# Loads asked for one head ahead, kq doubled on ScalarE, and value products spread over two pairs, in the attention of an encoder kernel

## The chip, the cores and the metric

The kernel runs on one core of a Trainium2 chip. The metric is the device time of one execution in microseconds (us). A core has four compute engines, each with its own queue in program order: TensorE (PE), VectorE (DVE), ScalarE (ACT) and GpSimd (POOL). A fifth, SyncE (SP), only issues DMA transfers. Engines wait for each other by semaphores; an instruction that waits holds everything behind it in its queue.

## The reference

Two encoder layers on 1024 positions of width 1024; attention and a convolution branch run side by side, then a gated feed-forward part with a short convolution:

```python
for l in range(2):
    p = rmsnorm(x, g_mix[l]) @ w_in[l]
    q = (rmsnorm(p[..., :384], g_q[l]) @ w_uq[l]).reshape(b, s, 8, 64 + 32)
    kv = (rmsnorm(p[..., 384:640], g_kv[l]) @ w_ukv[l]).reshape(b, s, 8, 64 + 64)
    q_nope, q_rope = q[..., :64], apply_rope(q[..., 64:])
    k_nope, v = kv[..., :64], kv[..., 64:]
    k_rope = apply_rope(p[..., 640:672])              # one for all heads
    sc = (q_nope . k_nope + q_rope . k_rope) / sqrt(96)   # per head, 1024 x 1024
    y_attn = softmax(sc) @ v
    u = silu(layernorm(dwconv31(a * sigmoid(gate))))
    x = x + concat(y_attn, u) @ w_o[l]
    z = dwconv3(rmsnorm(x, g_ffn[l]) @ w_up[l])
    x = x + (silu(z_gate) * z_value) @ w_down[l]
return rmsnorm(x, g_final)
```

## The kernel before

All instructions are put into the engines' queues by one Python program; its order is the order of each queue. Values of full precision are kept as a high and a low half (16-bit, or a rounded 32-bit pair), so that a product of two is several 16-bit products.

The change is in `attention`, which runs once per layer: about 190 of 2220 us, twice. Each of 8 heads has 8 **query tiles** of 128 queries, taken as 4 **pairs** (p = 0 to 3), 32 pairs in all. For a pair the steps are:

- `begin` and `scores`: for each of the two tiles a **whole product** of four 128x512 matmuls (line 1860, tiles k and q), and for both a **rest product** of four 32-row matmuls (L1867), which adds what is left of the rotary part. Its operand kq has to lie in rows 0 to 63 and again in rows 64 to 127; `again` copies it (L2066). The scores of a tile lie in a wide PSUM buffer, of which there are two.
- `largest`: the row maximum on DVE (L1878); `expo`: the exponential on ACT (L1886), which also sums the rows.
- `turn(pair, c)`, c = 0 to 3: four PE transposes (L1904) into a PSUM bank, of both tiles' probabilities for two key tiles; `upper` (ACT, L1912) writes the high half pt, `lower` (DVE, L1916) the low half. There are four such banks, shared with other users.
- `values(group, c)`: a **group** is two pairs, a half head. Two matmuls (L1932) of high halves for each c, and after c = 3 eight 64-column ones (L1937) for the low halves; then the output y is taken out by ACT (L1943) and DVE (L1944).
- `sums(h)`: reciprocal on DVE (L1954), written to memory (sd, L1955) and read back broadcast (rb, L1956), both by SP; POOL multiplies y by rb (L1965) `Y_DELAY` tiles later, and y is split into high and low (ys) on ACT (L233) and POOL (L235).

The main loop begins the scores of pair + 1 and turns `pair`. In between it issues side work by an agenda of due times (`others`): taps of the convolution on POOL (L2169 to L2174), sums of the layer norm (lns, L2180), output weights wo (L1000, L214, L215). `products(n)` issues one value step per tile: two in each pair, and in every second pair the eight closing matmuls.

The transfers of a head's k, q and kq are issued on SP by `load_head`, through the helper `move` (L159), from memory copies kd, qd and qrd. kq has three buffers, k and q two each. `load(h + 1)` stands in `begin` at p = 1 of head h. The tables `ROWS_FIRST` to `ROWS_LATE` say when the eight row tiles of v are made (`rows`, L1833).

Of the kernel before, what the change touches and what calls it, by code (L numbers as in the profile page):

```python
# [64 lines left out]
FFN_BANKS = (2, 4)  # L65
SIDE_TIME = 56
TOTAL_TIME = 57
Y_DELAY = 3
SUMS_AT = 8
Y_LAST = 4  # L70
Y_SPLIT = 8
# [79 lines left out]
class Encoder:  # L151
# [421 lines left out]
    def project(self, l, carry):  # L573
# [205 lines left out]
        def query_rope(i):  # L779
            p = ps[f"u{i}"]  # L780
            c, s = self.blk(f"rc{l}_{i}"), self.blk(f"rs{l}_{i}")
            for o, t in ((c, st["cos"]), (s, st["sin"])):
                nc.vector.tensor_tensor(out=by_parity(o), in0=in_order(p), in1=in_order(t), op=ALU.mult)
            st["rope", i] = c, s
            yield 2.44, 0.0
            if i == 0:
                return
            (c1, s1), (c2, s2) = st.pop(("rope", 0)), st.pop(("rope", 1))
            nc.vector.tensor_tensor(out=c1, in0=c1, in1=s2, op=ALU.subtract)
            nc.vector.tensor_tensor(out=c2, in0=c2, in1=s1, op=ALU.add)  # L790
            two = [self.blk(f"qr{l}_{i}", F16, (128, 2, T)) for i in range(2)]
            for hl, o in zip(two, (c1, c2)):
                nc.scalar.copy(out=hl[:, 0], in_=o)
            yield 2.5, 1.0
            for i, (hl, o) in enumerate(zip(two, (c1, c2))):
                nc.vector.scalar_tensor_tensor(out=hl[:, 1], in0=o, scalar=1.0, in1=hl[:, 0], op0=ALU.mult, op1=ALU.subtract)
                yield 1.25, 0.0
                self.move(qrd[i].rearrange("h d p t -> (h d) p t"), hl)
            for i, hl in enumerate(two):
                mine = hl[0:HALF]  # L800
                for e in range(2):
                    self.move(heads[0][2][e * ROPE + i * HALF:e * ROPE + (i + 1) * HALF], mine[:, 0, HALVES[e]])
                for p in range(2):
                    at = NOPE + i * ROPE + p
                    self.move(heads[0][0][at:at + ROPE - 1:2, 1], mine[:, p])

        def query(j):
            n = self.blk(f"qn{l}_{j}")
            nc.vector.tensor_tensor(out=by_parity(n), in0=in_order(ps[f"n{j}"]), in1=in_order(st["rq"]), op=ALU.mult)  # L809
            hl = self.blk(f"qns{l}_{j}", F16, (128, 2, T))  # L810
            nc.scalar.copy(out=hl[:, 0], in_=n)
            yield 1.22, 1.5
            nc.vector.scalar_tensor_tensor(out=hl[:, 1], in0=n, scalar=1.0, in1=hl[:, 0], op0=ALU.mult, op1=ALU.subtract)
            for h in range(DIRECT if j == 0 else 0):
                mine = hl[h * NOPE:(h + 1) * NOPE]
                self.move(heads[h][0][NOPE:128, 0], mine[:, 0])
                self.move(heads[h][0][0:NOPE], mine)
            if j:
                self.move(qd[2 * j:2 * j + 2].rearrange("h d p t -> (h d) p t"), hl)
            if j == 1:  # L820
                self.load_rope(heads[1], 1, qrd)
            yield 1.25, 0.0

# [995 lines left out]
    def attention(self, l, u, conv, away, spill, kvs, loaded, ahead, wo, begun):  # L1819
# [29 lines left out]
        def scores(pair):  # L1849
# [18 lines left out]
                                         stop=(e == 0), skip_group_check=True)  # L1868

            whole(0)  # L1870
            rest()
            return lambda: whole(1)

        def largest(n):
            h, qt = divmod(n, 8)
# [39 lines left out]
            hi, lo = halves(pair, c)  # L1915
            nc.vector.scalar_tensor_tensor(out=lo, in0=tps.pop((pair, c)), scalar=P_SCALE, in1=hi, op0=ALU.mult, op1=ALU.subtract)  # L1916

        def values(group, c, n):
# [10 lines left out]
            y, rb, po = st["y"], st["rb"], st["po", gg] if c < 3 else st.pop(("po", gg))  # L1929
            pt = st["pt"][gg][c // 2]  # L1930
            for i in range(2):
                nc.tensor.matmul(po, v[2 * c + i][:, h // 2, e, :], pt[0][:, 2 * (c % 2) + i, :],  # L1932
                                 start=(c == 0 and i == 0), stop=False, skip_group_check=True)
            if c == 3:
                for kt in range(8):
                    rows = slice(kt % 2 * 64, kt % 2 * 64 + 64)
                    nc.tensor.matmul(po[rows], v[kt][:, h // 2, e, main], st["pt"][gg][kt // 4][1][:, kt % 4, :],  # L1937
                                     start=False, stop=(kt >= 6), skip_group_check=True)
            if c < 3:
                return  # L1940
            st["pt"].pop(gg)
            qs = HALVES[gg]
            nc.scalar.activation(out=y[main, qs], in_=po[aux, :], func=AF.Copy, scale=vr[aux, 0:1])  # L1943
            nc.vector.scalar_tensor_tensor(out=y[main, qs], in0=po[main, :], scalar=vr[main, 0:1], in1=y[main, qs], op0=ALU.mult, op1=ALU.add)  # L1944
# [85 lines left out]
        chain = defaultdict(list)  # L2030
        for g in range(2 * HEADS - 1):
            for c in range(4):
                chain[4 * g + 4 + c].append((g, c))
        g = 2 * HEADS - 2
        chain[total - 2], chain[total - 1] = [(g, 2), (g, 3)], []
        chain[total], chain[total + 1] = [], []
        agenda[total].append(lambda: self.conv_split(l))
        agenda[total].append(begun["turn"])
        second = {}

        def products(n):
            for g, c in chain.get(n, ()):
                values(g, c, n)

        def others(n):
            for f in agenda.pop(n, ()):
# [1 line left out]

        def begin(pair):
            h, p = divmod(pair, 4)  # L2050
            if h >= HEADS:
                return
# [3 lines left out]
            second[pair] = scores(pair)  # L2056
            if p == 1 and h + 1 < HEADS and h + 1 not in loaded:
                loaded[h + 1] = load(h + 1)

        def each(pair, f, *e):  # L2060
            if pair < total // 2:
                f(*e)

        def again(h):
            qc = loaded[h][2]
            nc.vector.tensor_copy(out=qc[NOPE:128], in_=qc[0:NOPE])  # L2066

        for tt in ROWS_FIRST:
            rows(tt)()
        again(0)  # L2070
        begin(0)
        ends = [rows(tt) for tt in ROWS_SECOND]
        largest(0)
        second.pop(0)()
        expo(0)
        for f in ends:
            f()
# [6 lines left out]
        others(0)  # L2084
        for pair in range(total // 2 - 1):
            n, nxt = 2 * pair + 1, pair + 1
            products(n)
            begin(nxt)
            turn(pair, 0)
            upper(pair, 0)  # L2090
            turn(pair, 1)
            upper(pair, 1)
            largest(2 * nxt)
            ends = [rows(tt) for tt in ROWS_LATE.get(n, ())]
            turn(pair, 3)
# [12 lines left out]
            upper(pair, 2)  # L2108
            expo(2 * nxt + 1)
            lower(pair, 2)  # L2110
            lower(pair, 3)
            for f in ends:
                f()
            others(n + 1)
            for qi in range(2):
                state[pair // 4]["p"].pop(2 * (pair % 4) + qi)
            if pair % 4 == 2 and pair // 4 + 1 < HEADS:
                again(pair // 4 + 1)
        pair = total // 2 - 1
        early(0, range(3))  # L2120
        for c in range(4):
# [4 lines left out]
                others(total - 1 + c // 2)  # L2126
            if c == 1:
                early(1, range(2))
        g = 2 * HEADS - 1
        values(g, 0, total)  # L2130
        values(g, 1, total)
        early(1, range(2, 3))
        values(g, 2, total)
        values(g, 3, total)
        for m in range(2):
            early(m, range(3, 4))
            early_add(m)
# [179 lines left out]
```

## Time and profile before

| | us |
|---|---|
| median of three runs | 2224.16 |
| their range | 2217.61 to 2225.51 |
| the profiled execution | 2221.62 |
| its span | 2219.9 |
| attention, layer 0 | about 217 to 406 |
| attention, layer 1 | about 1317 to 1505 |

The page gives busy times of engines and groups of instructions; `<-` names what an instruction reads, and the idle time ahead of a group is put down to what ended it. Two more groups of the attention, which set the other engines' load (busy us, mean ns, idle ahead and its cause):

```profile
L1886 ACT ACTIVATE p<-s,mx 128x1024 f32<-128x1024 f32 x128 | 143.2, 1119 | 14.7 <-DVE mx L1878 14.4
L1912 ACT ACTIVATE pt<-t 128x512 f16<-128x512 f32 x256 | 140.0, 597 | 86.6 <-PE t L1904 86.1
```

### The profile page before, as it was taken

The page shows a single profiled execution, that of the slowest core. Times are in us where ns is not written, and L with a number is a line of the kernel's source. Part 1 is how long each engine was busy: PE and PEld are TensorE (multiplying, and loading weights), DVE is VectorE, ACT ScalarE, POOL GpSimd, SP SyncE. Part 2 cuts the span into 40 slices and gives each one's busy share as a digit, 9 for nine tenths or more (in the row PEclk, how much of TensorE's full clock was granted, in tenths as well). Part 3 has the DMA queues.
Part 4 walks back from the last instruction along what each step waited for, and adds up shares of the span by engine and source line. Part 5 has one row for each costly group of instructions (what it writes and reads, how often), then busy time and mean ns, then how long its engine had stood idle before and what let it go on. Part 6 is the DMA issues. An engine that isn't in the chain of part 4 may idle for free.

```text
span 2219.9 us, 29937 instructions
## 1 busy us (share of the span) xinstructions
PE 2173.6 (98%) x10708; PEld 1247.2 (56%) x10708; DVE 1855.9 (84%) x2547; ACT 1454.7 (66%) x2183; POOL 540.8 (24%) x534
## 2 busy tenths in 40 slices
PE   9999898999999999999999999999999999999998
PEld 7886454664444444644488865557544444446445
DVE  6988898888998887787859788888799888878877
ACT  6464787745888886554623657777468988865554
POOL 1223578301112111000012255762112121110000
PEclk9999999999999999999999999999999999999999
DMA  6897678845589786554578986878546888856533
GB/s 191 186 190 196 139 145 180 260 119 111 127 252 262 220 259 175 182 176 157 157 185 161 181 197 126 162 158 247 145 116 145 243 253 235 243 139 215 181 124 121
DMA packets 170758, 402.81 MB, mean 181 GB/s; under 512 B 25584, under 2 KB 34800, under 8 KB 170608
## 3 DMA queue, kind: packets, MB, share of 16 engines
q0 software_dynamic: 62528, 145.89, 35.9%
q1 hardware_dynamic: 107792, 254.47, 33.7%
q8 instruction: 84, 1.38, 0.3%
q14 instruction: 66, 0.54, 0.1%
q10 hardware_dynamic: 288, 0.53, 0.1%
HBM read 272.46 MB, written 67.56 MB: 153 GB/s over the span
## 4 chain that ended last, share of the span: by engine, by line
PE 86%; ACT 5%; DMA 3%; SPq 3%; DVE 2%; issue 1%; DVEq 0%; ACTq 0%
PE p L1324 35%; PE pd L1569 18%; PE po L1044 7%; PE t L1904 3%; PE pq L251 3%; PE pa L251 3%; ACT p L1886 2%; SPq L159 2%; PE pkv L251 2%; PE pg L251 2%; PE s L1860 2%; ACT pt L1912 2%; PE pn L251 1%; DMA q<-qrd 1%; PE pg L570 1%
## 5 line engine op out<-in xcount | busy, mean ns | idle before, releaser
L1324 PE MATMUL p<-b,w 128*128 128x512 f16 x3696 | 800.0, 379 | 0.2
L1324 PEld LDWEIGHTS <-w 128*128 128x128 f16 x3696 | 358.8, 98 | 431.8 <-issue 0.8
L1569 PE MATMUL pd<-ab,wd 128*128 128x512 f16 (+2 forms) x1920 | 404.2, 373 | 0.0
L1214 POOL DMA_DIRECT2D wu<-in_w_up x176 | 152.7, 882 | 766.8 <-DVE w L1288 576.5
L1569 PEld LDWEIGHTS <-wd 128*128 128x128 f16 x1656 | 161.9, 98 | 179.3 <-issue 0.5
L1912 ACT ACTIVATE pt<-t 128x512 f16<-128x512 f32 x256 | 140.0, 597 | 86.6 <-PE t L1904 86.1
L1878 DVE TENSOR_REDUCE mx<-s 128x1 f32<-128x1024 f32 x128 | 155.4, 1214 | 29.7 <-PE s L1860 19.6
L1288 DVE SCALAR_TENSOR_TENSOR w<-wu,wf,w 128x512 f16<-128x512 f32 (+1 forms) x216 | 177.2, 834 | 3.6 <-ACT w L1285 3.6
L1916 DVE SCALAR_TENSOR_TENSOR pt<-t,pt 128x512 f16<-128x512 f32 x256 | 165.0, 683 | 9.4 <-ACT pt L1912 7.3
L1285 ACT ACTIVATE w<-wu,wf 128x512 f16<-128x512 f32 (+1 forms) x216 | 164.8, 781 | 0.6 <-DMA wu<-in_w_up 0.6
L1860 PE MATMUL s<-k,q 128*128 128x512 f16 x512 | 136.3, 387 | 17.2 <-DMA q<-qrd 11.8
L1886 ACT ACTIVATE p<-s,mx 128x1024 f32<-128x1024 f32 x128 | 143.2, 1119 | 14.7 <-DVE mx L1878 14.4
L1558 ACT ACTIVATE ab<-ac,ds 128x512 f16<-128x512 f32 x108 | 75.5, 717 | 108.5 <-DVE ac L1473 72.9
L2169 POOL TENSOR_SCALAR late<-gate,par 128x1019 f32<-128x1019 f32 (+13 forms) x99 | 136.4, 1378 | 27.7 <-DVE qn L809 14.7
L1904 PE MATMUL t<-ident,p 128*128 128x128 f32 x1024 | 141.2, 282 | 1.7 <-DVE pt L1916 1.6
L2152 DVE SCALAR_TENSOR_TENSOR conv<-gate,par,conv 128x1009 f32<-128x1009 f32 (+14 forms) x110 | 139.9, 1274 | 3.2 <-ACT conv L665 0.4
L1904 PEld LDWEIGHTS t<-ident,p 128*128 128x128 f32 x1024 | 117.8, 144 | 31.8 <-issue 12.3
L1784 DVE SCALAR_TENSOR_TENSOR o<-zg,par,o 128x1023 f32<-128x1023 f32 x88 | 112.8, 1282 | 8.9 <-ACT o L1778 7.4
L1332 DVE SCALAR_TENSOR_TENSOR zg<-p,wf,zg 128x512 f32<-128x512 f32 x72 | 54.0, 750 | 70.9 <-PE p L1324 61.3
L1784 DVE SCALAR_TENSOR_TENSOR v<-zv,par,v 128x1023 f32<-128x1023 f32 x88 | 112.1, 1276 | 0.0
L1559 DVE SCALAR_TENSOR_TENSOR ab<-ac,ds,ab 128x512 f16<-128x512 f32 x108 | 79.9, 748 | 19.2 <-ACT ab L1558 19.2
L1230 ACT ACTIVATE wsq<-wu 128x1024 f16<-128x1024 f32 x88 | 92.1, 1047 | 0.0
(2180 smaller groups left out, 3831.7 us busy)
## 6 DMA issues: line engine op xcount, KB each, us to landing
wu<-in_w_up SPq DMA_DIRECT2D x98, 512.0 KB, 4.6
wu<-in_w_up POOLq DMA_DIRECT2D x176, 256.0 KB, 4.9
sd<-in_w_down SPq DMA_DIRECT2D x44, 512.0 KB, 7.5
ws<-sd SPq DMA_DIRECT2D x44, 512.0 KB, 5.4
act<-v SPq DMA_DIRECT2D x36, 512.0 KB, 4.7
ac<-act SPq DMA_DIRECT2D x72, 256.0 KB, 4.9
wo<-in_w_o POOLq DMA_DIRECT2D x32, 256.0 KB, 7.2
x_mix<-y SPq DMA_DIRECT2D x32, 256.0 KB, 3.4
```

Source lines behind the costliest of these rows:

```text
L251: nc.tensor.matmul(ps[:, HALVES[c]], w, x[:, HALVES[c]], start=(k == 0 and s == 0), stop=(k == n - 1 and s == 2))
L1285: nc.scalar.activation(out=t, in_=src, func=AF.Copy, scale=scale[f])
L1288: nc.vector.scalar_tensor_tensor(out=t, in0=src, scalar=scale[f], in1=hi, op0=ALU.mult, op1=ALU.subtract)
L1324: nc.tensor.matmul(ps, w[p][:, k * 128:(k + 1) * 128], b[:, q], start=(i in (1, 5, 2) and k == 0 and t == 0), stop=(k == 3 and t == 2), sk ...
L1569: nc.tensor.matmul(ps[t, m][:, cs], w[i, j][p][:, m * 128:(m + 1) * 128], b[:, q, cs], start=(i in (1, 5, 2) and j == 0 and s == 0), stop= ...
L1784: self.nc.vector.scalar_tensor_tensor(out=o[:, a:b], in0=z[:, at + a:at + b], scalar=self.par[l][:, tap:tap + 1], in1=o[:, a:b], op0=ALU.m ...
L1860: nc.tensor.matmul(two[e][:, cs], q[:, i, at[e]], k[:, i, cs], start=(i == 0 and e == 0), stop=(i == 1 and e == 1), skip_group_check=True)
L1878: nc.vector.tensor_reduce(out=mx, in_=st["s"][qt], op=ALU.max, axis=AX.X, negate=True)
L1886: nc.scalar.activation(out=p, in_=ps, func=AF.Exp, bias=mx, accum_out=st["sums"][:, qt:qt + 1])
L1904: nc.tensor.transpose(tp[:, i, qi * 128:(qi + 1) * 128], st["p"][2 * qp + qi][:, kt * 128:(kt + 1) * 128], self.ident)
L1912: nc.scalar.activation(out=halves(pair, c)[0], in_=tps[pair, c], func=AF.Copy, scale=P_SCALE)
L1916: nc.vector.scalar_tensor_tensor(out=lo, in0=tps.pop((pair, c)), scalar=P_SCALE, in1=hi, op0=ALU.mult, op1=ALU.subtract)
```

## The change

1. `load(h + 1)` is asked for at p = 0 of head h instead of p = 1.
2. `again` runs on ScalarE instead of VectorE.
3. The rest product no longer directly follows the first whole product: it comes after the first turn of the pair before. Two of the four value steps of a group stand at the start of the pair that follows it, one in its middle, and one late in the pair before; the eight closing matmuls (`values_end`) start the next pair.
4. Four row tiles of v come first instead of three, none late in the loop. At the start of a layer, head 0's rotary and plain q go directly to its tiles ahead of the spill to qrd, and the rest rows of head 1 are loaded at step 3.
5. `Y_DELAY` is 5 instead of 3.

```diff
-Y_DELAY = 3
+Y_DELAY = 5
...
-ROWS_FIRST, ROWS_SECOND, ROWS_THIRD = (0, 1, 2), (3, 4), (5, 6)
-ROWS_LATE = {2: (7,)}
+ROWS_FIRST, ROWS_SECOND, ROWS_THIRD = (0, 1, 2, 3), (4, 5), (6, 7)
...
             whole(0)
-            rest()
-            return lambda: whole(1)
+            return rest, lambda: whole(1)
...
-            if p == 1 and h + 1 < HEADS and h + 1 not in loaded:
+            if p == 0 and h + 1 < HEADS and h + 1 not in loaded:
                 loaded[h + 1] = load(h + 1)
...
-            nc.vector.tensor_copy(out=qc[NOPE:128], in_=qc[0:NOPE])
+            nc.scalar.copy(out=qc[NOPE:128], in_=qc[0:NOPE])
...
         for pair in range(total // 2 - 1):
             n, nxt = 2 * pair + 1, pair + 1
-            products(n)
+            group, odd = divmod(pair - 2, 2)
+            if odd and group >= 0:
+                values_end(group, n)
+            elif group >= 0:
+                values(group, 3)
+                values(group, 1)
             begin(nxt)
             turn(pair, 0)
+            after[nxt].pop(0)()
+            turn(pair, 1)
             upper(pair, 0)
-            turn(pair, 1)
             upper(pair, 1)
             largest(2 * nxt)
-            ends = [rows(tt) for tt in ROWS_LATE.get(n, ())]
             turn(pair, 3)
+            lower(pair, 0)
+            after[nxt].pop(0)()
+            largest(2 * nxt + 1)
             upper(pair, 3)
-            second.pop(nxt)()
-            lower(pair, 0)
-            largest(2 * nxt + 1)
+            if not odd and group >= 0:
+                values(group, 2)
             expo(2 * nxt)
+            others(n)
+            turn(pair, 2)
             lower(pair, 1)
-            for f in ends:
-                f()
-            others(n)
-            products(n + 1)
-            ends = [rows(tt) for tt in ROWS_LATE.get(n + 1, ())]
-            turn(pair, 2)
             upper(pair, 2)
             expo(2 * nxt + 1)
+            if odd:
+                values(group + 1, 0)
             lower(pair, 2)
             lower(pair, 3)
-            for f in ends:
-                f()
             others(n + 1)
```

In the rows below s_h_t are the scores of head h, tile t; t_h_pc turn c of pair p; p_h_t the probabilities; o_h_g the values of group g; pt_ab a high (0) or low (1) half of half b of the keys. Between PE's rows stand its weight loads, left out. First PE before, head 4, from the last value product ahead of pair 1's scores to the second whole product:

```order
L1932 MATMUL o_3_1_2843<-pt_00_2735,v_2_1653 128x512
...
L1860 MATMUL s_4_2_2864<-k_0_1324,q_4_2586 128x512
...
L1867 MATMUL s_4_2_2864<-kq_1326 128x512
L1867 MATMUL s_4_3_2865<-kq_1326 128x512
...
L1904 MATMUL t_4_00_2886<-ident,p_4_0_2837 128x128 x2
L1904 MATMUL t_4_00_2886<-ident,p_4_1_2852 128x128 x2
L1904 MATMUL t_4_01_2896<-ident,p_4_0_2837 128x128 x2
...
L1860 MATMUL s_4_3_2865<-k_0_1324,q_4_2586 128x512
```

And PE after the change, the same place (line numbers of the changed kernel are two or so higher):

```order
L1932 MATMUL o_3_1_2863<-pt_01_2744,v_6_1730 128x512
...
L1932 MATMUL o_3_1_2863<-pt_00_2742,v_2_1653 128x512
...
L1862 MATMUL s_4_2_2878<-k_0_1324,q_4_2517 128x512
...
L1905 MATMUL t_4_00_2884<-ident,p_4_0_2845 128x128 x2
L1905 MATMUL t_4_00_2884<-ident,p_4_1_2861 128x128 x2
...
L1869 MATMUL s_4_2_2878<-kq_1326 128x512
L1869 MATMUL s_4_3_2879<-kq_1326 128x512
...
L1905 MATMUL t_4_01_2893<-ident,p_4_0_2845 128x128 x2
...
L1862 MATMUL s_4_3_2879<-k_0_1324,q_4_2517 128x512
```

The first turn's four transposes now stand between the whole product and the rest product, and two value steps instead of one stand ahead of the pair.

SP before, around the load of head 3 (k<-kd, q_3<-qd, kq<-qrd), with the sums of head 1 (sd, rb):

```order
L159 DMA kq_1326<-qrd_81 16x512 x4
L159 DMA q_2_2012<-qrd_81 32x1024 x2
L1955 DMA sd_1622<-sums_1_1940 128x8
L1956 DMA rb_0_1846<-sd_1622 64x1024
L159 DMA k_1_1325<-kd_82 64x1024 x3
L159 DMA q_3_2299<-qd_80 64x2048
L159 DMA q_3_2299<-qd_80 64x1024
```

And SP after the change:

```order
L1959 DMA sd_1622<-sums_0_1670 128x8
L1960 DMA rb_0_1854<-sd_1622 64x1024
L158 DMA k_1_1325<-kd_82 64x1024 x3
L158 DMA q_3_2231<-qd_80 64x2048
L158 DMA q_3_2231<-qd_80 64x1024
L158 DMA kq_1326<-qrd_81 16x512 x4
L158 DMA q_3_2231<-qrd_81 32x1024 x2
L1959 DMA sd_1622<-sums_1_1940 128x8
```

The load of head 3 now stands ahead of sd and rb of head 1 instead of behind them, with those of head 0 next ahead of it.

DVE before, where kq is copied in the queue between the low halves of the one pair and the maximum of the next (lines as in the kernel):

```order
L1916 SCALAR_TENSOR_TENSOR pt_11_2167<-t_1_22_2198,pt_01_2166 128x2x256
L1916 SCALAR_TENSOR_TENSOR pt_11_2167<-t_1_23_2177,pt_01_2166 128x2x256
L2066 COPY kq_1326<-kq_1326 64x512
L1944 SCALAR_TENSOR_TENSOR yt_0_1845<-o_1_0_2131,sc_85,yt_0_1845 64x512
L1878 TENSOR_REDUCE mx_2_0_2247<-s_2_0_2225 128x1
```

ACT after the change, the same place:

```order
L1913 ACTIVATE pt_01_2173<-t_1_22_2199 128x2x256
L1887 ACTIVATE p_1_7_2206,sums_1_1940<-s_1_7_2152,mx_1_7_2189 128x1024
L2053 COPY kq_1326<-kq_1326 64x512
L1947 ACTIVATE yt_0_1853<-o_1_0_2139,sc_85 64x512
L1913 ACTIVATE pt_00_2171<-t_1_30_2243 128x2x256
```

The copy now follows the second exponential on ACT and stands ahead of the next pair's first high half.

More of the change, by code (lines that the diff above doesn't have):

```diff
@@ L797, in query_rope @@
                 yield 1.25, 0.0
[L798 to L802, printed above, removed]
                 for p in range(2):
                     at = NOPE + i * ROPE + p
-                    self.move(heads[0][0][at:at + ROPE - 1:2, 1], mine[:, p])
+                    self.move(heads[0][0][at:at + ROPE - 1:2, 1], hl[0:HALF, p])
+            st["two"] = two
         def query(j):
@@ L2029, in attention @@
             agenda[TOTAL_TIME + i - 1].append(lambda i=i: self.conv_total(l, conv, i))
[L2030 to L2036, printed above, removed]
         agenda[total].append(lambda: self.conv_split(l))
         agenda[total].append(begun["turn"])
[L2039 to L2043, printed above, removed]
+        after = {}
         def others(n):
@@ L2055, in begin @@
                             "s": {}, "p": {}, "pt": {}, "qk": loaded.pop(h)}
[L2056 to L2057 removed]
+            after[pair] = list(scores(pair))
+            if p == 0 and h + 1 < HEADS and h + 1 not in loaded:
                 loaded[h + 1] = load(h + 1)
[L2060 to L2062 removed]
         def again(h):
             qc = loaded[h][2]
[L2066 removed]
+            nc.scalar.copy(out=qc[NOPE:128], in_=qc[0:NOPE])
         for tt in ROWS_FIRST:
@@ L2071, in attention @@
         begin(0)
+        after[0].pop(0)()
         ends = [rows(tt) for tt in ROWS_SECOND]
         largest(0)
-        second.pop(0)()
+        after[0].pop(0)()
         expo(0)
```

57 lines of the change are left out of this document (33 added, 24 removed).

## The prediction

> **What bounds the kernel now.** I read the page's busy line first, then the busy time of each engine in the stretch that the diff touches (the attention of the first layer), then the groups of instructions with the idle time before them.
>
> ```profile
> PE 2173.6 (98%) x10708; PEld 1247.2 (56%) x10708; DVE 1855.9 (84%) x2547; ACT 1454.7 (66%) x2183; POOL 540.8 (24%) x534
> 217.00:406.00 189.00, 172.93 (x1075) 98.14 (x1074) 160.90 (x211) 144.34 (x264) 126.63 (x101) 0.97 0.77 159
> L1860 PE MATMUL s<-k,q 128*128 128x512 f16 x512 | 136.3, 387 | 17.2 <-DMA q<-qrd 11.8 <-DMA q<-qd 3.1 <-issue 1.3
> L1867 PE MATMUL s<-kq 32*128 32x512 f16 x256 | 43.7, 401 | 18.5 <-DVE kq L2066 10.7 <-ACT p L1886 7.7
> ```
>
> PE (TensorE) is busy 98% of the span, so only what stops PE, or spreads its instructions out, costs time. In the attention the columns are PE, weight loads, DVE, ACT and POOL: PE is busy 172.9 of 189.0 us, 91%. Two groups hold the idle time: the score products wait for a head's transfers (11.8 + 3.1 = 14.9 us) and for the doubled rest rows kq (10.7), over both layers. Next, the pace: the turns (transposes) of pair 1 and of pair 30, in each layer, and two undisturbed pairs.
>
> ```profile
> 224.59 1.53 PE L1904 MATMUL t<-ident,p 128*128 128x128 f32 x12
> 408.18 1.53 PE L1904 MATMUL t<-ident,p 128*128 128x128 f32 x12
> ...
> 1325.31 1.42 PE L1904 MATMUL t<-ident,p 128*128 128x128 f32 x11
> 1507.18 1.53 PE L1904 MATMUL t<-ident,p 128*128 128x128 f32 x12
> ```
> ```profile
> 289.28 1.53 PE L1904 MATMUL t<-ident,p 128*128 128x128 f32 x12
> 290.64 1.03 PE L1860 MATMUL s<-k,q 128*128 128x512 f16 x4
> 291.51 0.59 PE L1932 MATMUL o<-pt,v 128*128 128x512 f16 x2
> 291.94 0.60 PE L1904 MATMUL t<-ident,p 128*128 128x128 f32 x4
> ...
> 298.36 1.05 PE L1937 MATMUL o<-pt,v 128*64 128x512 f16 x8
> 299.34 1.04 PE L1860 MATMUL s<-k,q 128*128 128x512 f16 x4
> 300.31 0.39 PE L1867 MATMUL s<-kq 32*128 32x512 f16 x4
> 300.64 1.53 PE L1904 MATMUL t<-ident,p 128*128 128x128 f32 x12
> ```
>
> Twenty-nine pairs take 183.6 and 181.9 us. Two undisturbed pairs take 300.64 − 289.28 = 11.36, and 29 pairs at half of that 164.7; so 18.9 + 17.2 = 36.1 us are waits and what follows them. The starts also give the length of each piece: 12 transposes 1.36 (four 0.45), whole product 0.87, two value products 0.43, the eight that end a group 0.98, rest product 0.33.
>
> **Load one head ahead.**
>
> ```profile
> 231.77 1.03 PE L1860 MATMUL s<-k,q 128*128 128x512 f16 x4
> ...
> 262.21 1.01 PE L1860 MATMUL s<-k,q 128*128 128x512 f16 x2 [3.07 <-DMA q<-qd]
> 263.48 1.01 PE L1860 MATMUL s<-k,q 128*128 128x512 f16 x2 [0.26 <-DMA q<-qrd]
> ```
> ```profile
> 249.52 0.47 SPq L1956 DMA_DIRECT2D rb<-sd  x1
> 250.08 3.10 SPq L159 DMA_DIRECT2D k<-kd  x3
> ...
> 260.03 0.98 SPq L159 DMA_DIRECT2D q<-qrd  x2
> ```
>
> PE asks for head 2's tiles at 262.21 − 3.07 = 259.14. Their issues on SP run from 250.08 to 261.01, behind rb, which has to wait until sd has landed. The k tile that they overwrite is read last by the product that ends at 231.77 + 1.03 = 232.80. In the new order they stand ahead of sd and rb: they can start near 233, and 10.9 of issues plus 2.5 to the landing (261.01 to 263.48) end near 246.5, some 12 us ahead of need. The 14.9 us go; I take **−15**. Delayed in turn are sd and rb, by up to 13 us; their reader is POOL's product y·rb, which Y_DELAY also moves two tiles (a pair) on. It is needed only by the output projection, so that costs nothing except at the end (below).
>
> After such waits PE runs at half clock.
>
> ```profile
> 206.50:213.30 6.80, 6.09 (x16) 0.50 0.96 271
> 261.10:267.90 6.80, 5.43 (x21) 0.50 0.09 25
> 335.20:342.10 6.90, 4.25 (x31) 1.00 0.96 190
> 1339.70:1343.10 3.40, 3.40 (x14) 0.50 1.03 190
> ```
> ```profile
> 337.94 0.59 PE L1860 MATMUL s<-k,q 128*128 128x512 f16 x2 [2.65 <-DMA q<-qrd]
> 1338.57 0.49 PE L1867 MATMUL s<-kq 32*128 32x512 f16 x3 [1.48 <-DVE kq L2066]
> ```
>
> In the windows of PE alone (PE busy, granted clock, DMA share, GB/s) the granted clock is 0.50 for 6.8 us behind the load wait at 261, for 3.4 behind the kq wait of 1.48 us, and 1.00 behind a wait of 2.65. Behind the load waits I find 17.1 us at half clock in all, which cost at most half, 8.5. Some of it was hidden by waits inside it: **−6** (0 to −8.5).
>
> The Trainium skill ("TensorE: Matmul & The Clock Gate", section "Part 1: The HAM clock gate") says the clock is halved after an idle free-running window of about 3.4 us, and advises no PE-idle gaps over that. The rows differ: half clock follows 1.48 and 3.07 and does not follow 2.65. By that rule no wait here would be the cause, and the clock term would be 0.
>
> **kq doubled on ACT.**
>
> ```profile
> L2066 DVE COPY kq<-kq x16: 285/726/1910, 205.6 to 1484.4; 64x512 f16<-64x512 f16 x16
> L1943 ACT ACTIVATE yt<-o,sc 64x512 f32<-64x512 f32 x32 | 21.9, 683 | 3.1 <-PE o L1937 2.4
> 207.21 0.61 PE L1867 MATMUL s<-kq 32*128 32x512 f16 x3 [2.96 <-DVE kq L2066]
> 1309.10 0.61 PE L1867 MATMUL s<-kq 32*128 32x512 f16 x3 [2.76 <-DVE kq L2066]
> ```
>
> Sixteen copies of 285 to 1910 ns, median 726, leave DVE. What one takes on ACT the trace does not show; the nearest row is ACT's 64x512 eviction, 683 ns, so I take 0.7, between 0.3 (DVE's fastest) and 1.9 (its slowest). Of the waits of 10.7 us, 2.96 + 2.76 = 5.7 stand at the two starts; the other 5.0 are in later heads, where kq came late because its load did and DVE's queue held it. With loads 12 us ahead they go, with the 3.4 us at half clock behind one of them (at most 1.7). On the other side fourteen copies of 0.7 stand in ACT's queue between exponentials; if ACT sets the pace, they cost 14 × 0.7 = 9.8, less what ACT has idle. Taken: **−3** (−6.7 to +4).
>
> The Trainium skill speaks against this edit: "ScalarE: Activation LUTs", "Rules for kernel authors", puts plain elementwise work on VectorE, up to three times faster. Its ACTIVATE price, 186 ns + 0.833 per element, gives an estimate of 613 ns for 512, and the sum would be 1.2 us lower.
>
> **The new order inside a pair.** PE's work is the same. What moves: the first turn no longer stands behind the rest product, value products no longer fill the same places, and rest stands behind turn 0.
>
> ```profile
> 294.73 1.53 PE L1904 MATMUL t<-ident,p 128*128 128x128 f32 x12
> ...
> 295.43 1.57 ACT L1912 ACTIVATE pt<-t 128x512 f16<-128x512 f32 x3 [1.06 <-PE t L1904]
> ...
> 299.52 0.20 ACT L1886 ACTIVATION_READ_ACCUMULATOR p<-s,mx 128x1 f32 x1
> ```
>
> ACT's round (copies, exponential, copy, exponential) runs 295.43 to 299.72, 4.3 us, and then waits for PE: rest, and four transposes of which the first copy needs all (0.70 behind the turn's start: 0.45 of transposes, 0.25 to hand over). In the new order only two of the four are left when the second exponential ends, about 0.1 + 0.22 + 0.25 = 0.6, and the second copy waits some 0.3 for rest: 5.1 to 5.2 a pair on ACT. PE's own pieces, by their lengths, make 2 × 1.81 + 4 × 0.87 + 4 × 0.43 + 0.98 + 2 × 0.33 = 10.5, with the 0.1 to 0.2 that whole products lose ahead of a rest 10.6. ACT's y eviction of a group (0.68) comes on top in each second pair, of which I let 0.4 delay the copies: 5.4 + 5.5 = 10.9 for two pairs. Gain (11.36 − 10.9) × 14.5 × 2 = **−13** (PE's own 10.6 gives −22; above it nothing bars a loss, and the same 0.3 the other way is +10).
>
> With PE waiting for ACT and DVE on each pair, their side work costs. In the stretch quoted at the top DVE is busy 160.9, and fifteen times two undisturbed pairs are 15 × 10.12 = 151.8 by the row below, so 9.1 us a layer of other work, and on ACT 144.3 − 15 × 9.35 = 4.1.
>
> ```profile
> 289.28:300.64 11.36, 11.12 (x75) 6.38 (x73) 10.12 (x15) 9.35 (x17) 9.84 (x9) 1.00 0.99 184
> ```
>
> Most of it fits into what a pair leaves free (10.9 − 10.1 on DVE): **+4** (0 to +16).
>
> **Starts and ends.** At the two starts four row tiles run ahead of the scores instead of three, kq is fetched first and doubled on ACT: the 5.7 us of waits go largely (−4), with the half clock behind them (6.8 + 3.4, at most 5.1; of it −2.5). Against that the seventh and eighth row tiles no longer fill pairs: +2.5 for the idle that they covered. Sum **−4** (−9 to +3). At the end:
>
> ```profile
> 399.75 2.35 POOL L235 TENSOR_TENSOR ys_5l<-yt,ys_5h 128x1024 fp32r<-128x1024 f32 x1 [9.48 <-ACT ys_5h L233]
> 414.92 0.39 PE L1044 MATMUL po_e<-ys_5l,wo 128*128 128x512 f32 x1
> ```
>
> ys_5l is ready at 402.10 and first used at 414.92, a spare 12.8. Two tiles later and behind three sums (up to 8 us) it still fits; what can slip are the same splits of earlier heads: **0** (0 to +3).
>
> **Sum.** −15 − 6 − 3 − 13 + 4 − 4 = −37. Against the profiled execution's own 2221.6 (span 2219.9 and 1.7 around it; 2.5 under the median 2224.2, inside the spread of 2217.6 to 2225.5) that is 2184.6; I say **2184**.
>
> **Rivals.**
>
> - *Only the waits go* (0.18): loads and kq as above, but the pace stays at 11.36, since ACT's round and DVE's together fill it. −15 − 6 − 3 + 4 − 4 = −24: 2198. For it: DVE is busy 10.12 of 11.36.
> - *PE sets the pace* (0.12): 10.6 for two pairs, side work hidden: −15 − 6 − 3 − 22 − 4 = −50: 2172. For it: PE was already busy 11.12 of 11.36.
> - *The change doesn't bring the transfers earlier* (0.06): SP's queue is held by its first k issue, or the transfers take longer beside other DMA (share 0.99 in the undisturbed pairs), so the load waits stay and only the pace and the starts gain: −13 + 4 − 4 = −13: 2208.
> - *The clock stays* (0.04): half-clock stretches are not tied to these waits, so the 6 and the 2.5 remain: 2192.
> - *Slower: DVE's queue decides* (0.05).
>
> ```profile
> 298.30 1.88 DVE L1916 SCALAR_TENSOR_TENSOR pt<-t,pt 128x512 f16<-128x512 f32 x3
> 300.47 0.74 DVE L1944 SCALAR_TENSOR_TENSOR yt<-o,sc,yt 64x512 f32<-64x512 f32 x1 [0.29 <-ACT yt L1943]
> ```
>
> DVE's lowers and y stand in one queue with the maxima that the exponentials wait for. If lowers 2 and 3 (1.3) and y (0.74) end after the next pair's scores, each maximum comes that much later, then the exponential, the turn, and again the lowers: a closed round. Slack is about 0.5; the 36 us of waits are eaten when a pair is 36 / 58 = 0.6 longer, so from 1.1 us of lateness on. At the full 2.0 us a pair is 0.9 over 5.68 and the kernel 58 × 0.9 − 37 + 13 = +28 slower: near 2250.
>
> **How the numbers follow.** My forecast holds 0.55. The range takes in the rivals at 2198 and 2172 and the clock's, stretched by the side work (+6 over 2198) and the pace (−4 under 2172): 2168 to 2204. Left out are the transfers that come no earlier, the slower case, and as much again of surprises of size. With 0.5% as what a measurement can tell, the line is 2213: faster 0.91, same 0.05, slower 0.04 (the slower rival's mild form falls into same).
>
> **What would show it.** Idle before L1860 put down to q or k falls from 15 to under 2, and before the rest product from kq by 5 or more in later heads; SP's k issues stand ahead of sd; granted clock 1.00 from the third pair on; two undisturbed pairs between 10.6 and 11.1; a copy of kq on ACT near 0.7. The prediction is wrong if maxima wait in DVE's queue with their scores done, if ACT's copies wait for nothing while PE idles, or if new PE waits for exponentials exceed 0.4 a pair.

## The result, and the profile after

The changed kernel takes 2189.76 us (median of four runs, 2188.32 to 2192.46) against 2224.38 for the kernel before (2217.61 to 2225.51): ratio 0.9852, 95% interval 0.983 to 0.9874, or 34.6 us less. The forecast was 2184 with a range of 2168 to 2204. The profiled execution has a span of 2190.7 against 2219.9, so the two profiles account for 29.2 us. A profile is of one run: that of the kernel after is of the slowest of its four, with half clock at the end of both layers, and those of o1 and u2 below are of the fastest of theirs.

The page's busy line, the busy time of each engine between the turns of pair 1 and pair 30 in the first layer, and the groups of PE with their idle time, all of the kernel after:

```profile
PE 2157.8 (98%) x10708; PEld 1245.1 (57%) x10708; DVE 1839.9 (84%) x2531; ACT 1471.1 (67%) x2199; POOL 540.4 (25%) x534
218.92:385.58 166.66, 160.73 (x1044) 94.46 (x1043) 150.45 (x196) 146.70 (x258) 122.93 (x101) 1.00 0.81 170
L1862 PE MATMUL s<-k,q 128*128 128x512 f16 x512 | 131.8, 380 | 2.3 <-ACT p L1887 2.3
L1869 PE MATMUL s<-kq 32*128 32x512 f16 x256 | 29.0, 384 | 1.1 <-ACT kq L2053 1.1
L1905 PE MATMUL t<-ident,p 128*128 128x128 f32 x1024 | 151.3, 278 | 11.0 <-ACT p L1887 6.0 <-DVE pt L1917 4.2 <-DVE v L1848 0.8
L1932 PE MATMUL o<-pt,v 128*128 128x512 f16 x256 | 65.7, 379 | 8.6 <-DVE pt L1917 8.6
```

The 29 pairs take 166.66 us where they took 183.59. No product waits for a DMA any more, kq is waited for 1.1 us instead of 10.7, and the granted clock of the stretch is 1.00. New are waits of the turns (11.0) and of the value products (8.6, for an output bank). SP's queue, where head 2 is loaded:

```profile
227.31 2.02 SPq L158 DMA_DIRECT2D k<-kd  x3
...
235.38 0.90 SPq L158 DMA_DIRECT2D q<-qrd  x2
237.26 0.34 SPq L1959 DMA_DIRECT2D sd<-sums  x1
240.62 0.45 SPq L1960 DMA_DIRECT2D rb<-sd  x1
```

The load is issued by 236.3, ahead of sd and rb, and first used at 252.0. The pace of undisturbed pairs, by PE's first score product of pairs 12, 14 and 16:

```profile
274.96 0.60 PE L1862 MATMUL s<-k,q 128*128 128x512 f16 x2
...
286.55 0.39 PE L1862 MATMUL s<-k,q 128*128 128x512 f16 x1
...
297.50 0.60 PE L1862 MATMUL s<-k,q 128*128 128x512 f16 x2
```

The last two pairs of head 3 take 10.95 us, the first two 11.59. Then the end of the first layer's attention, PE and DVE, and PE alone in a window behind it (busy, granted clock, DMA share, GB/s):

```profile
385.58 0.38 PE L1905 MATMUL t<-ident,p 128*128 128x128 f32 x2
387.17 0.44 PE L1905 MATMUL t<-ident,p 128*128 128x128 f32 x2 [1.21 <-ACT p L1887]
...
390.09 0.60 PE L327 MATMUL rc_0s<-ident,rc 128*128 128x128 f32 x4
392.81 0.63 PE L1905 MATMUL t<-ident,p 128*128 128x128 f32 x4 [2.12 <-DVE pt L1917]
```
```profile
391.00 1.06 DVE L1966 SCALAR_TENSOR_TENSOR yt<-yt,rb 64x512 f32<-64x512 f32 x1
391.99 0.68 DVE L1917 SCALAR_TENSOR_TENSOR pt<-t,pt 128x512 f16<-128x512 f32 x1
394.25:397.65 3.40, 3.40 (x10) 0.50 1.11 281
```

In the last pair the last turn waits 2.12 us for a bank. Low half 1 gives it free, which stands on DVE behind a product y·rb; the spread of the reciprocals (rc) took another bank. Half clock follows. The kernel before had no wait here and ran its last value products in this place:

```profile
410.85 1.03 PE L1932 MATMUL o<-pt,v 128*128 128x512 f16 x4
411.81 1.05 PE L1937 MATMUL o<-pt,v 128*64 128x512 f16 x8
412.79 0.65 PE L1904 MATMUL t<-ident,p 128*128 128x128 f32 x4
```

### The profile page after: what moved, and what is told of

Its sections match the earlier page's. It is cut to its first block, busy times and chain, and to the rows that moved or that the text cites. A ratio compares the mean times of both kernels' runs of the same rounds, so it can differ in the third digit from the quotient of the medians.

```text
span 2190.7 us, 30030 instructions
## 1 busy us (share of the span) xinstructions
PE 2157.8 (98%) x10708; PEld 1245.1 (57%) x10708; DVE 1839.9 (84%) x2531; ACT 1471.1 (67%) x2199; POOL 540.4 (25%) x534
## 3 DMA queue, kind: packets, MB, share of 16 engines
q1 hardware_dynamic: 107792, 254.47, 34.1%
## 4 chain that ended last, share of the span: by engine, by line
PE 87%; ACT 6%; DVE 4%; issue 2%; DMA 1%; SPq 0%; DVEq 0%; ACTq 0%
PE p L1326 36%; PE pd L1571 18%; PE po L1046 7%; PE pq L250 3%; PE pa L250 3%; PE t L1905 3%; ACT p L1887 2%; PE s L1862 2%; PE pkv L250 2%; PE pg L250 2%; PE o L1932 2%; DVE mx L1879 2%; PE pn L250 1%; PE pg L569 1%; ACT pt L1913 1%
## 5 line engine op out<-in xcount | busy, mean ns | idle before, releaser
L1917 DVE SCALAR_TENSOR_TENSOR pt<-t,pt 128x512 f16<-128x512 f32 x256 | 164.2, 679 | 10.7 <-ACT pt L1913 10.3
L1905 PE MATMUL t<-ident,p 128*128 128x128 f32 x1024 | 151.3, 278 | 11.0 <-ACT p L1887 6.0
L1862 PE MATMUL s<-k,q 128*128 128x512 f16 x512 | 131.8, 380 | 2.3 <-ACT p L1887 2.3
```

The lines of the kernel that those rows point to most:

```text
L1862: nc.tensor.matmul(two[e][:, cs], q[:, i, at[e]], k[:, i, cs], start=(i == 0 and e == 0), stop=(i == 1 and e == 1), skip_group_check=True)
L1905: nc.tensor.transpose(tp[:, i, qi * 128:(qi + 1) * 128], st["p"][2 * qp + qi][:, kt * 128:(kt + 1) * 128], self.ident)
```

## The experiments

Times are medians; each was measured beside the kernel before in the same session (2220.7 to 2224.4).

| kernel | us | ratio to before, 95% |
|---|---|---|
| after | 2189.8 | 0.9852 (0.983 to 0.9874) |
| u1: after, load at p = 1 | 2217.2 | 0.9978 (0.9967 to 0.9989) |
| u4: as u1, sums two tiles later | 2191.3 | 0.986 (0.984 to 0.9879) |
| b1: before, load at p = 0 | 2200.9 | 0.9902 (0.9883 to 0.9921) |
| o1: after with the old loop | 2189.7 | 0.9865 (0.9849 to 0.9881) |
| g2: as o1, kq by DMA | 2188.5 | 0.9856 (0.9842 to 0.9871) |
| u2: after, kq copied on DVE | 2196.9 | 0.9888 (0.9869 to 0.9906) |
| u3: after, Y_DELAY 3 | 2192.7 | 0.9869 (0.9851 to 0.9887) |
| s1: after, three row tiles first | 2190.5 | 0.9855 (0.9837 to 0.9874) |
| f1: after, late side work in the last pair | 2187.7 | 0.9847 (0.9831 to 0.9864) |
| f6: f1 and kq by DMA | 2178.0 | 0.9802 (0.9781 to 0.9822) |
| g1: after, all side work late, kq by DMA | 2180.3 | 0.9817 (0.9802 to 0.9832) |
| f8: after, last pair old, kq by DMA | 2175.3 | 0.9798 (0.9783 to 0.9812) |

### The load order

```diff
-            if p == 0 and h + 1 < HEADS and h + 1 not in loaded:
+            if p == 1 and h + 1 < HEADS and h + 1 not in loaded:
```

u1 undoes it in the kernel after, b1 makes the same edit the other way in the kernel before.

> The changed kernel with the load of the next head asked for at p = 1 again, all else kept. If the load order is what removed the 14.9 us of waits, they come back (about 15 us idle ahead of the score products, put down to q), with half clock behind some of them (up to 6 us): 2205 to 2212 us, against 2190 for the changed kernel. Rival: the new order inside the pair hides the transfers anyway; then the time stays within 3 us of 2190 and the score products show no wait on a DMA.

> The kernel before with one edit, the load of the next head asked for at p = 0. By the terms of the prediction the load waits (14.9 us) and the half clock behind them (6) go, and with them most of the kq waits in later heads (5.0): 22 to 26 us off 2222, so 2196 to 2200. Rival, from the run that undid only this (it cost 27 us): the load order and the new order inside the pair hang together, and alone each gives less; then 2203 to 2212.

u1 cost 27.5 us, more than its forecast; b1 gained 19.8, just short of its own. The group of whole products in u1, and SP's queue there ahead of head 7:

```profile
L1862 PE MATMUL s<-k,q 128*128 128x512 f16 x512 | 135.6, 385 | 27.1 <-DMA q<-qrd 21.9 <-ACT p L1887 3.8 <-DMA q<-qd 1.4
```
```profile
361.54 0.34 SPq L1959 DMA_DIRECT2D sd<-sums  x1
362.95 0.45 SPq L1960 DMA_DIRECT2D rb<-sd  x1
363.83 2.75 SPq L158 DMA_DIRECT2D k<-kd  x3
```

The waits are back, and larger than before (21.9 + 1.4 = 23.3 against 14.9): the rest of the change without the load order is worth 5 us (2222.3 to 2217.2), and the load order is worth 20 in the old loop and 27 in the new. With the waits comes more half clock, 27.3 us in u1's two loops against 20.5 in the kernel before, and ACT's copy waits 9.8 us for the transfer of kq and holds ACT's queue meanwhile (DVE's copy waited 6.7 in the kernel before). A reading that no run isolates is that quicker pairs also meet the same late load sooner.

Two things hang on p = 0: the load is asked for a pair earlier, and it stands ahead of sd and rb. u4 keeps p = 1 and moves the sums instead:

```diff
+            if p == 1 and h + 1 < HEADS and h + 1 not in loaded:
...
-SUMS_AT = 8
+SUMS_AT = 10
```

> The changed kernel with the load asked for at p = 1 again, but with the sums of the head before moved two tiles later, so that on SP the load still stands ahead of sd and rb. If what counts is that the load no longer waits behind rb (which waits for sd to land, and sd for DVE), the load waits stay away: within 3 us of 2190. Rival: the whole pair of lead (5.5 us) is needed; then waits of 1 to 3 us a head return, 2200 to 2217.

```profile
341.35 2.92 SPq L158 DMA_DIRECT2D k<-kd  x3
...
349.36 0.96 SPq L158 DMA_DIRECT2D q<-qrd  x2
357.38 0.34 SPq L1959 DMA_DIRECT2D sd<-sums  x1
```
```profile
L1862 PE MATMUL s<-k,q 128*128 128x512 f16 x512 | 131.7, 380 | 2.3 <-ACT p L1887 2.3
```

SP's queue where head 7 is loaded, and the group of u4: no wait on a DMA, and 2191.3 us. So it is the place ahead of sd and rb that counts; the pair of lead is not needed. It was not even had: SP runs ahead of PE, and the first k issue for head 2 starts at 227.1 in u4 and at 227.3 in the kernel after, ahead of the pairs that it stands with in the program (235.3 and 229.5). The "one head ahead" of the title is one pair earlier in the program, and the loads come earlier because sd and rb no longer stand in front of them.

### The copy of kq

u2 puts the copy back on DVE. f6 brings kq by DMA to both places instead, on top of f1 below:

```diff
-                self.move(qc[e * ROPE + i * HALF:e * ROPE + (i + 1) * HALF], qrd[i, h][:, 0, HALVES[e]])
+                for c in range(2):
+                    at = c * NOPE + e * ROPE + i * HALF
+                    self.move(qc[at:at + HALF], qrd[i, h][:, 0, HALVES[e]])
...
-            if pair % 4 == 2 and pair // 4 + 1 < HEADS:
-                again(pair // 4 + 1)
```

> The changed kernel with kq doubled on DVE again, all else kept. In the changed kernel the ACT copy (0.62 us) stands ahead of the y eviction and of the next high halves in the first pair of a head, and that pair takes 6.01 to 6.15 us against 5.37 to 5.58 for the others. If the copy on ACT is what lengthens it, the first pairs shrink by about 0.4 and the time falls by 14 x 0.4 = 6 us to 2184. Rival: with the loads early, DVE's copy (0.29) delays the maximum behind it as much; then the time stays within 2 us of 2190. Second rival: moving the copy was a gain; then 2194 or more.

> The changed kernel with the side work of the last pair issued later (as in f1_end_order, 2.1 us faster than the changed kernel) and with kq brought by DMA to both places instead of doubled by an ACT copy, except for head 0. If the copy on ACT lengthens the first pair of each head by 0.4 to 0.6, that goes: 14 x 0.45 = 6 us, so 2181 to 2183. Rival: four more transfers a head delay q and rb on SP, or the first pair is long for another reason (the y eviction and the output bank); then 2186 to 2190.

```profile
L1869 PE MATMUL s<-kq 32*128 32x512 f16 x256 | 32.0, 384 | 9.5 <-DVE kq L2053 9.5
```

In u2 (its group of rest products) the kq waits return, 9.5 us, 4.6 of it at the two starts, and the time rises by 7 by the medians: the second rival. The profiles show 1.4 of the 7. The copy on ACT is the better of the two, but not free: f6 is 9.6 us under f1, 0.69 for each of the 14 copies. Of this 8.3 lies in the loop, 0.59 a copy, near the copy's own 0.617. f6's first product of pairs 12 and 14 shows the first pairs of a head at the pace of the others, 10.95:

```profile
272.78 1.04 PE L1864 MATMUL s<-k,q 128*128 128x512 f16 x4
...
283.73 0.39 PE L1864 MATMUL s<-k,q 128*128 128x512 f16 x1
```

b1 shows where the old waits came from. With the loads early the rest products of the old loop still wait:

```profile
L1867 PE MATMUL s<-kq 32*128 32x512 f16 x256 | 45.4, 387 | 22.5 <-DVE kq L2066 13.7 <-ACT p L1886 7.9 <-DMA q<-qd 1.0
```

13.7 us for kq, 5.6 of it at the two starts and 8.1 in later heads, against 5.7 and 5.0 in the kernel before: the late load did not cause them. What did can be read from the copies. In later heads every wait for kq follows a copy that took 719 ns or more, and these are copies beside which POOL computes. The longest, and one with POOL idle, both in u2:

```profile
1338.33 2.32 POOL L2165 TENSOR_TENSOR conv<-conv,late 128x1016 f32<-128x1016 f32 x1
1338.48 2.31 DVE L2053 COPY kq<-kq 64x512 f16<-64x512 f16 x1
1340.85 0.49 PE L1869 MATMUL s<-kq 32*128 32x512 f16 x3 [1.88 <-DVE kq L2053]
...
1387.35 0.29 DVE L2053 COPY kq<-kq 64x512 f16<-64x512 f16 x1
```

Four profiles hold 50 such copies on DVE (before, b1, u2, g2). Fifteen have no POOL computation beside them and take 285 to 289 ns. The other 35 take 294 to 2315 ns, and each ends 0.15 us after a POOL instruction ends. On ACT every copy takes 616 to 618 ns, whatever POOL does. What a copy takes over 0.29 us makes up 3.7 of the 5.0 us of waits in later heads before, 6.9 of 9.0 in b1 (with one of 0.96 that the page puts down to a q transfer) and all 5.0 in u2; the rest is the copy's place in DVE's queue. No run takes POOL's work away, so that POOL holds the copy is read from these times alone.

### The order of the loop

o1 is the kernel after with the loop of the kernel before, and keeps all other edits:

```diff
-            if odd and group >= 0:
-                values_end(group, n)
...
+            products(n)
             begin(nxt)
             turn(pair, 0)
-            after[nxt].pop(0)()
-            turn(pair, 1)
             upper(pair, 0)
+            turn(pair, 1)
...
             turn(pair, 3)
             upper(pair, 3)
+            second.pop(nxt)()
             lower(pair, 0)
```

> The changed kernel with the loop of the kernel before (value products two a pair, rest product right behind the first whole product); load order, ACT copy, start and Y_DELAY as changed. From the two profiles the new order gains 13 us between the turns of pair 1 and pair 30 and loses 12.7 behind them. If both belong to the order, they come back together and the time stays within 3 us of 2190. Rival: the loss at the end belongs to Y_DELAY and the moved side work, and only the gain goes; then 2200 to 2204.

2189.7 against 2189.8: by the medians the new order gives nothing on balance. The stretches of the profiles, both layers added, from starts of PE's rows: (a) first score product to the turns of pair 1, (b) from there to the turns of pair 30, (c) from there to the last matmul of the layer's output projection (L1044 before):

| us | a | b | c |
|---|---|---|---|
| before | 42.0 | 365.5 | 198.3 |
| b1 | 41.6 | 346.5 | 198.2 |
| o1 | 34.1 | 339.0 | 199.2 |
| g2 | 37.9 | 334.3 | 199.3 |
| after | 31.7 | 333.3 | 210.9 |
| u4 | 31.7 | 333.4 | 207.9 |
| f1 | 32.7 | 333.4 | 205.8 |
| f6 | 31.6 | 325.1 | 205.8 |
| f8 | 31.7 | 329.0 | 198.7 |

From o1 to after the start gains 2.4 and the loop 5.7, and the end loses 11.7, so between the profiles after is 4 us behind o1. Of the 11.7 the half clock makes 3.0: u4 has the same loop, end and waits of 2.12 us, but no half clock, and its (c) is 207.9. The old loop's own pace, two pairs of o1:

```profile
334.22 1.04 PE L1863 MATMUL s<-k,q 128*128 128x512 f16 x4
...
345.58 0.60 PE L1863 MATMUL s<-k,q 128*128 128x512 f16 x2
```

11.36, as before; the new order does bring 10.95, and the ACT copy takes part of it back in each first pair.

g2 is o1 with kq by DMA, and with head 0's copy on DVE rather than ACT.

> As o1_old_loop, but kq comes by DMA to both places (no copy in the loop except head 0). In the old loop the rest product waits about 1 us in several heads for the copy, wherever it stands in a queue. If that is what the copy costs, 6 to 9 us go: 2181 to 2184, and the new order with the same edit (2178) is only 3 to 6 better. Rival: ACT and DVE set the old loop's pace, and the copy's place is filled by them; then within 3 us of o1_old_loop.

1.2 us less. By the profiles the loop (b) gains 2.4 and 2.3 us, and the start loses 2.9 and 0.9 with the DVE copy: the rest product at the first start waits 2.43 instead of 0.79. So in the loop the DMA is worth 4.7 us in the old order and 8.3 in the new one (f1 to f6).

### The end, the delay and the start

f1 issues the side work of the last pair behind the last turn:

```diff
-            others(n)
+            if pair < total // 2 - 2:
+                others(n)
             turn(pair, 2)
             lower(pair, 1)
             upper(pair, 2)
+            others(n)
```

> The changed kernel with the side work of the last pair of the loop issued behind turn 2, lower 1 and upper 2 instead of ahead of them, all else kept. If that order causes the wait of 2.12 us ahead of the last turn (it waits for a bank that lower 1 gives free, behind a y multiplication of 1.06 on DVE, and the spread of the reciprocals takes a bank too), the wait goes in both layers, and the half-clock stretch behind it (3.41 us, 1.7 us lost): 2 x 3.8 = 7.6 us, 2182. Rival: the wait is set by the maximum and the exponential of the last scores, so it stays at 1.5 to 2 us at the next step: 2188 or more.

2.1 us less by the medians, and 4.5 by the profiles: the half clock went, but 1.14 us of the wait moved to the spread of the reciprocals, behind the same DVE queue. f8 runs the last pair in the old order, with rest first, and the last value products ahead of the last turn; kq comes by DMA:

```diff
+            if pair == total // 2 - 2:
+                after[nxt].pop(0)()
...
+                others(n)
+                values(group, 2)
+                values_end(group, n + 1)
+                turn(pair, 2)
```

> The changed kernel with kq by DMA, and with the last pair of the loop alone in the order of the kernel before (rest first, the last value products and the eight closing ones ahead of the last turn). If the missing filler ahead of the last turn is what the end lost, its waits (1.14 left in f6_end_and_dma) and the rest of the lead over the kernel before go: 1 to 2 us a layer, 2174 to 2176. Rival: the end waits for the casts on ACT in the pair ahead; then 2178 or more.

```profile
383.45 1.53 PE L1907 MATMUL t<-ident,p 128*128 128x128 f32 x12
...
386.12 0.59 PE L1934 MATMUL o<-pt,v 128*128 128x512 f16 x2
386.65 1.05 PE L1946 MATMUL o<-pt,v 128*64 128x512 f16 x8
387.85 0.63 PE L1907 MATMUL t<-ident,p 128*128 128x128 f32 x4 [0.15 <-PE o L1946]
```

2175.3, the fastest, 14.5 us under the change. The closing value products cover what DVE needs, and stretch (c) is back at 198.7. Not all of that is gain: the last turns now start behind the rest product, so (b) holds 3.9 us more than in f6, and (b) and (c) together fall by 3.2.

g1 issues all side work behind the second exponential:

```diff
-            others(n)
             turn(pair, 2)
             lower(pair, 1)
             upper(pair, 2)
             expo(2 * nxt + 1)
+            others(n)
```

> The changed kernel with kq by DMA and with the side work of every pair issued behind the second exponential instead of ahead of it. If the casts and weight copies on ACT are what delays that exponential (0.56 us in two pairs a layer and 1.21 in the last one), those waits shrink to under 0.2: about 4 us under f6_end_and_dma, 2174. Rival: the casts then hold the next pair's first high half as long; then 2178 or more.

2180.3, slower than f6 by 2.3: the rival's time, but not its reason. By the profiles its loop (b) is 2.1 us shorter over both layers than f6's, with 1.9 us of waits for exponentials ahead of the turns instead of 6.0, but its end (c) is 2.1 longer and its start (a) 0.9.

u3 and s1 undo two small parts:

```diff
-Y_DELAY = 5
+Y_DELAY = 3
...
-ROWS_FIRST, ROWS_SECOND, ROWS_THIRD = (0, 1, 2, 3), (4, 5), (6, 7)
+ROWS_FIRST, ROWS_SECOND, ROWS_THIRD = (0, 1, 2), (3, 4), (5, 6, 7)
```

> The changed kernel with Y_DELAY = 3 as before, all else kept. In the changed kernel the cast of ys_5h (1.03 us on ACT) falls into the last pair of the loop, ahead of an exponential for which PE waits 1.21 us, in both layers. If the delay causes that, the wait shrinks to about 0.2 and the time falls by some 2 us to 2188. Rival: the wait comes from the exponentials' place itself; then the 1.21 stays and the time is within 1 us of 2190.

> The changed kernel with three row tiles of v ahead of the first scores instead of four, and three instead of two in the third place, all else kept. If the fourth tile is what covers the wait for kq at the start, that wait grows by up to its 1.36 us in each layer, to about 2, with 1 to 3 us of half clock behind it: 2192 to 2197. Rival: the wait is set by the transfer of kq, asked for earlier now, and the moved tile takes its time elsewhere; then within 1.5 us of 2190.

u3 is 2.9 us slower by the medians (1.2 by the profiles): the turns wait less for exponentials, 4.4 us against 6.0 (the wait of 1.21 in the last pair is 0.27), but the loop is longer by 1.2 and 1.5. The delay moves the casts' cost rather than making it. s1 is the same within the spread: the fourth row tile is not what shortened the start. Its stretch (a) is 34.4, 2.7 over the kernel after, because the tile that each layer there runs ahead of the stretch now stands in it.

## Why the prediction came out as it did

The total was right, within 6 us, and part of that is luck. By the profiles the loop, stretch (b), lost 32.2 us where its terms (−15, −6, −3, −13, +4) make −33. The end cost 12.6 that the sum had at nothing, and the starts brought more than their −4.

- **Load one head ahead, −15 and −6.** Right in size: b1 alone gives 19.8, and there no load wait is left in the loop and the half clock is gone with the waits, from 20.5 us in the loops to none. Of the two reasons given, the place ahead of sd and rb is the one that counts (u4).
- **kq on ACT, −3.** The sign was right in the new loop (u2); in the old one no run moves the copy alone. The reasoning that the later heads' waits go because the load is early failed: in b1 they stay, 8.1 us. The reading of the kernel before was wrong here: in five heads DVE's copy waits for its transfer (6.7 us), and in none of these does the rest product wait for kq. What lengthened the copies was POOL's work beside them, by the times above, and on ACT they are free of it. The other half of the sum, 14 copies on ACT, was counted at some 4 of at most 9.8: f6 against f1 gives 9.6. The copy's length, taken as 0.7, is 0.617.
- **The pace, 10.9 for two pairs, −13.** The number was right where no copy stands, 10.95, but by luck. It came from a round of ACT for which PE waits. In f6 PE has no idle time at all in these pairs, while ACT is busy 9.72 and DVE 10.2 to 10.4 of 10.95. So PE sets the pace, as one of the rivals had it, and its own pieces take 10.95 in this order, not the 10.6 summed from lengths. Over 29 pairs the gain is 0.41 × 29 = 11.9 rather than 13. The loss of 10 named beside this term is a slip: 0.3 above 10.9 is 11.2, still a gain of 5.
- **Side work, +4.** From o1 to after stretch (b) falls by 5.7. The pace gives −11.9, and the ACT copies cost 8.3 − 4.7 = 3.6 more than in the old loop, which makes −8.3. The 2.6 left for side work, and whatever else the order changes, lie inside the range.
- **Starts, −4.** Right in kind, too small: stretch (a) lost 10.3 us, of which 2.7 is the row tile that now stands ahead of it. Of the 7.6 left, 2.4 come with the new loop (o1 to after). What remains is the earlier kq transfer, which no run isolates, and the ACT copy of head 0: a DVE copy there costs 3.8 (g2).
- **Ends, 0 (0 to +3).** This step failed. It looked at when ys_5l is ready and found room, and not at what PE does in the last pair. Stretch (c) lost 12.6 us, 3.0 of it half clock: a wait for an exponential behind a cast, a bank held by DVE's queue, and the fillers that had covered it gone. f8 takes that back.

The rival *only the waits go* had the pace wrong, but its verdict on the order holds: the load order and the place of the copy and of the start's transfers carry nearly all of the gain (o1 gives 31.6 us in its own session), and the new order adds nothing until its end is mended. The slower rival did not occur, though maxima do wait in DVE's queue with their scores done: by their rows half of the 128 start 0.04 us behind their scores, 60 more within 1 us, and four 1.1 to 1.8 behind. That rival begins to lose time when every pair is 1.1 late. Its price was also too low, as the waits gained are counted twice: 2.0 less a slack of 0.5 is 1.5 a pair, and 58 × 1.5 − 37 + 13 = +63, not +28.

The sentences on the Trainium skill ("ScalarE: Activation LUTs"): the rule in "Rules for kernel authors" that elementwise work belongs on VectorE would have put kq back on DVE, which is 7 us slower here (u2). Alone the copy is faster there, 285 to 289 ns against 617, but not beside POOL's work. The estimate of 613 ns for the ACT copy, from the ACTIVATE price in the section "What ACT_TABLE_LOAD costs", agrees with the 617 measured.

## What to carry to other kernels

Look at what a queue of transfers waits for, not only at when a transfer is asked for: here two small transfers, one of which waits for another engine, held the eleven of the next head. After a new loop order, read the last iteration by itself, as fillers that the steady state doesn't miss can be what covered the end. And price a small copy between dependent steps in its place, not by its length alone: here it cost nearly its full 0.617 us on ACT in the new loop and about half in the old one, and on DVE it took anything from 0.29 to 2.3. If there is time ahead, let the transfer write both places.

## What the runs showed of the hardware

The half clock of PE didn't follow the length of a pause alone. In u2 the same instruction waits 2.12 us in each layer; PE alone, first the two 3.41 us windows that end where the clock could change, then the stretches behind:

```profile
391.41 0.63 PE L1905 MATMUL t<-ident,p 128*128 128x128 f32 x4 [2.12 <-DVE pt L1917]
...
1481.72 0.52 PE L1905 MATMUL t<-ident,p 128*128 128x128 f32 x3 [2.12 <-DVE pt L1917]
```
```profile
389.14:392.55 3.41, 1.29 (x12) 1.00 1.05 371
1477.99:1481.40 3.41, 1.61 (x10) 1.00 1.09 323
```
```profile
392.60:395.90 3.30, 3.30 (x10) 0.50 1.10 291
1481.40:1484.80 3.40, 3.08 (x19) 1.00 1.09 348
```

The half-clock stretches of one execution start at whole multiples of 3.41 us from each other (in u2 392.55 and 1341.46: 278 × 3.413). The pause that fell into one such window whole (PE busy 1.29 us of 3.41) was followed by half clock, the one that ran over the window's end (1.61 busy) was not. That fits a clock set at the end of fixed windows by how busy PE was in them; it would also explain why a 2.65 us pause in the kernel before was not followed by half clock. It doesn't explain all: one pause of 1.48 was.

With windows of 3.413 us laid out from the half-clock starts of each of the fourteen profiles, and 20 us left out at both ends, there are 25 windows at full clock that half clock follows: in 24 of them PE is busy 0.29 to 1.53 us, in the one behind the 1.48 us pause 1.93. No other full-clock window has PE busy less than 1.61. Half clock goes on where PE is busy 2.69 us or less of a half-clock window, and ends from 3.07 on. So whether the same pause costs half clock hangs on where it falls: of the pauses of 2.12 us, one in each layer, half clock follows both in the kernel after, one in u2 and none in u4.

The Trainium skill ("TensorE: Matmul & The Clock Gate", section "Part 1: The HAM clock gate") has a free-running window of about 3.4 us, which agrees with the 278 × 3.413; that the window must be idle does not, since PE was busy 38% of the one that led to half clock.
